# First q, k and cache fetches of each attention stage on ScalarE's queue, and the work pool below the k and q pools

## The chip, the cores and the metric

The kernel runs on one core of a Trainium2 chip. The time is device microseconds of one launch. Five engines work side by side, each in its own order: TensorE (PE, matmuls), VectorE (DVE), ScalarE (ACT), GpSimd (POOL) and SyncE (SP, which only issues transfers). Transfers between HBM and SBUF are issued here by SP and, for a few outputs, by ACT.

## What the kernel must compute

One inference step of a two layer encoder for 2048 frames of a new stream and 64 frames of a running one, whose 256 past frames of keys and values come from a cache. Each layer is x + W_out(silu(gate) * mixer(RMSNorm(x))), with one input projection to q, k, v and gate. There are 4 heads of width 256, and the model is 1024 wide. Layer 0 mixes by differential attention, layer 1 by stick-breaking attention:

```python
# layer 0, per head: two softmax maps of 128 wide queries and keys
p = softmax(where(visible, q @ k * 128**-0.5, NEG_INF))   # two maps m
w = p[:, :, 0] - lam * p[:, :, 1]
o = w @ v
# layer 1
z = q @ k * 256**-0.5
a = where(earlier, exp(z + rev_cumsum(log_sigmoid(-z))), 0)
o = a @ v
```

New k and v rows are outputs too, and a final RMSNorm follows layer 1.

## The kernel before

All data lie transposed, features on the partitions. Float32 operands are split into a high and a low part (`split`, L47: ACT writes `hi`, at L49; DVE or POOL subtracts, at L50), and a product is three matmuls (`mm3`, L54 to L56). Each layer has three stages, one after the other:

- **p_phase** projects q, k, gate and v per head. The last projection of a layer is v of head 3: 17 blocks of 24 matmuls. Per block ACT evacuates the PSUM tile to a work tile `o1` or `o2` (L240), issues the store `out_v` on its own queue (L241) and makes the high part of the split tile `s` (L49); POOL makes the low part (L50); SP stores it to `vS` in HBM (L190). The split tiles have two buffers, `o1` and `o2` two each.
- **a_phase** runs over groups of four blocks of 128 queries (and, per head, first the 64 sample rows). `load` fetches q and k of a group (tiles `q`, `k`) from HBM, `values` fetches v, `past` the cache. In layer 0 the scores `s` go from PSUM to SBUF on DVE (L404, which also writes the small tile `st`), the exponentials run on ACT (L412), and the combined row is transposed on PE (`tp`, L468), split into `wh` and `wl` and multiplied with v (`o`). In layer 1 ACT evacuates the scores (tile `z`, L438). PSUM holds three score tiles. `mixed` (and in layer 0 `finish`, L525 to L538) normalises and gates a finished group in the tiles `sq`, `rm`, `rs` and `ot`, and SP stores `ot` to `oT` in HBM (L538, L544).
- **o_phase** reads `oT` back in chunks `oraw` of 128 features (three buffers, L709), splits each into `oh` and `ol` and multiplies with the output weights `wh`, `wl` (split from `wraw`, L697) into `ps`. It starts with the 512 frames of the attention's first two groups of frames; the frames of the last group come later. The second block of frames uses the other pair of `oh`, `ol`.

The program is written with tile pools: a pool takes a stretch of SBUF when it is opened, pools are stacked in the order in which they are opened, and a stage's pools lie over those of the stage before. A tile that lies over an older one waits until all readers and writers of the old one are done, transfers included. The instructions of each engine are put in order before the run, by a planner inside the framework that simulates the queues; so a change in one wait can move instructions elsewhere. SP and ACT share eight completion counters in turn: a new transfer waits until the transfer eight issues earlier has landed.

In the kernel before, all q, k, v and cache fetches are issued on SP (L336, L350, L372). The pools of the attention stage lie in the order v, weights `wh`/`wl`, gate, k, q, rows, and the work pool with `st`, `osc`, `sq`, `rm`, `rs`, `ot` last. The tile of the first k lies there over a work tile `o1` of the projection. The output stage of layer 0 opens a pad of 36 KB per partition first (L672).

Of the kernel before, what the change touches and what calls it, by code (L numbers as in the profile page):

```python
# [42 lines left out]
def pool(tc, name, bufs=1, **kw):  # L43
    return tc.tile_pool(name=name, bufs=bufs, reuse_waits="tile", **kw)


def split(nc, hi, lo, x, lo_eng):  # L47

    nc.scalar.activation(hi, x, AF.Copy)  # L49
    lo_eng.tensor_tensor(lo, x, hi.bitcast(F32), ALU.subtract)  # L50
# [263 lines left out]
def a_phase(tc, k, layer):  # L314
    nc = tc.nc
    ck, cv = k.ckT[layer], k.cv[layer]
    with ExitStack() as es:
        vp = es.enter_context(pool(tc, f"av{layer}", 4))
        wtp = es.enter_context(pool(tc, f"awt{layer}", 3))
        gp = es.enter_context(pool(tc, f"ag{layer}"))  # L320
        kp = es.enter_context(pool(tc, f"ak{layer}", 4))
        qp = es.enter_context(pool(tc, f"aq{layer}", 2))
        rbp = es.enter_context(pool(tc, f"arb{layer}", 2))
        rap = es.enter_context(pool(tc, f"ara{layer}", 8))
        wk = es.enter_context(pool(tc, f"aw{layer}", 1))
        psp = es.enter_context(pool(tc, f"aps{layer}", 2, space=PSUM))
        osc = None
        if layer == 0:
# [7 lines left out]
        def past(src, hi, lo):  # L336

            raw = qp.tile([P, 2, PAST], F32, tag="raw", name="raw", bufs=2)
            nc.sync.dma_start(out=raw, in_=src)
            split(nc, hi, lo, raw, nc.gpsimd)  # L340

        def rows(ap, h, c0, c1):
# [2 lines left out]
        def head_rows(ap, h, c0, c1):  # L345
            return ap[h * HW:(h + 1) * HW, :, c0:c1].rearrange("(m p) s t -> p s m t", p=P)

        def fetch(dst, src):
            for s in range(2):
                nc.sync.dma_start(out=dst[:, s], in_=src[:, s])  # L350

        def load_q(h, t0, n):
            t, hl = pair(qp, f"q{n}", [2, n], 2 if n == 512 else 1)
            fetch(t.bitcast(F32), head_rows(k.qS[layer], h, t0, t0 + n))
            return hl

        def load_k(h, g):
            t, hl = pair(kp, "k", [2, 512])
            if g is None:
                past(rows(ck, h, 0, PAST), t[:, 0, :, :PAST], t[:, 1, :, :PAST])  # L360
                fetch(t[:, :, :, PAST:PAST + NS].bitcast(F32), head_rows(k.kS[layer], h, SEQ, T))
            else:
                fetch(t.bitcast(F32), head_rows(k.kS[layer], h, g * 512, g * 512 + 512))
            return hl

        def load_v(h, g):
            hs = slice(h * HW, (h + 1) * HW)
            t, hl = pair(vp, "v", [4, HW])
            vs = k.vS[layer]
            if g is None:  # L370
                past(cv[:, hs].rearrange("(b p) e -> p b e", p=P), t[:, 0, :2], t[:, 1, :2])
                nc.sync.dma_start(out=t[:NS, :, 2].bitcast(F32), in_=vs[SEQ:T, :, hs])  # L372
            else:
                fetch(t.bitcast(F32), vs[g * 512:g * 512 + 512, :, hs].rearrange("(b p) s e -> p s b e", p=P))
            return hl
# [176 lines left out]
        def sums():  # L552
            return wk.tile([P, 4], F32, tag="s15", name="s15", bufs=4) if layer == 0 else None

        def load(i):
            if i < len(groups) and i not in loaded:
                h, g = groups[i]
                qt = load_q(h, SEQ, NS) if g is None else load_q(h, g * 512, 512)
                loaded[i] = (qt, load_k(h, g))
# [5 lines left out]
        def group(h, rows, s15, nq, kbs, wq, t0):  # L565
            u = K()
            u.last = (h, t0) == (H - 1, 3 * 512)
            u.h, u.rows, u.s15, u.nq, u.kbs, u.wq, u.t0, u.wts = h, rows, s15, nq, kbs, wq, t0, {}
            return u

        def all_units():
            for i, (h, g) in enumerate(groups):
                load(i)
                load(i + 1)
                qt, kt = loaded[i]
                if g is None:
                    row = rap.tile([P, 320], F32, tag="rs", name="rowS", bufs=1)
                    s15 = sums()
                    m, r = unit(row, 0, NS, qt, [(kt, PAST + NS, PAST + NS)], None if layer == 0 else k.smask, s15)
                    yield m, r, group(h, [row], s15, NS, [(i, 0, P, 0), (i, 1, P, 0), (i, 2, NS, 0)], NS, SEQ)  # L580
                    continue
                base = i - g
                full = [(loaded[base + c][1], 512, 512) for c in range(g)]
                per = {0: 4, 1: 2}.get(g, 1)
                wid = {0: 512, 1: 1024, 2: 2048, 3: 2048}[g]
                u_rows, s15 = [], sums()
                kbs = [(base + c, b, P, 0) for c in range(g) for b in range(4)]
                kbs += [(i, b, P, b) for b in range(4)]
                for j in range(4):
                    if j % per == 0:  # L590
                        slot = rap.tile([P, 2048], F32, tag="ra", name="rowA")
                    row = slot[:, (j % per) * wid:(j % per) * wid + wid]
                    u_rows.append(row)
                    m, r = unit(row, j, P, qt, full + [(kt, (j + 1) * P, max(256, (j + 1) * P))], k.mask[layer], s15)
                    yield m, r, group(h, u_rows, s15, P, kbs, 512, g * 512) if j == 3 else None

        def s_stream():

            prev, note = iter(()), None
            for m, r, nt in all_units():  # L600
                live = [m, prev]
                cost = [0.0, 0.0]
                while any(x is not None for x in live):
                    n = min((x for x in range(2) if live[x] is not None), key=lambda x: cost[x])
                    try:
                        c = next(live[n])
                        cost[n] += c
                        yield c
                    except StopIteration:
                        live[n] = None  # L610
                if note:
                    ready.append(note)
                prev, note = r, nt
            yield from prev
            ready.append(note)
# [134 lines left out]
def trunk(ctx: ExitStack, tc, xT, wqkg, wv, wo, small, ckT, cv, rope, masks, idn,  # L750
# [52 lines left out]
    with pool(tc, "rs0", side="right") as rp:  # L803
        p_phase(tc, k, 0, xT, rstd_tiles(rp))
    a_phase(tc, k, 0)
    with pool(tc, "rs1", side="right") as rp:
        rs = rstd_tiles(rp)
        k.acc = rp.tile([P, TT[0][1]], F32, name="acc")
        o_phase(tc, k, 0, xT, rs)
        p_phase(tc, k, 1, k.y1T, rs)  # L810
    a_phase(tc, k, 1)
    o_phase(tc, k, 1, k.y1T, None)

# [73 lines left out]
```

## Time and profile before

| | before |
|---|---|
| three runs | 2995.58, 3002.43, 3003.42 us |
| median | 3002.43 us |
| profiled execution | 3003.18 us, of which the span from the first to the last instruction is 3001.4 us |
| PE busy | 2888.2 us (96%) |
| DVE, ACT, POOL busy | 1683.0 us (56%), 1246.1 us (42%), 873.7 us (29%) |
| mean granted TensorE clock | 0.98 of full speed |

The stages follow one another: projection of layer 0 to 779 us, its attention to 1343 us, output and projection of layer 1 to 2285 us, its attention to 2801 us, and the output stage to the end. In the table "busy" is the time in which an engine executes; waiting is not in it. PE is the engine to watch: what it does not do at full clock is lost.

### The profile page before, as it was taken

How to read it: one execution, taken by the hardware profiler on the slowest of the kernel's cores; microseconds unless marked ns; L12 is line 12 of the kernel's file. 1: busy time of each engine (PE TensorE's matmuls, PEld its weight loads, DVE VectorE, ACT ScalarE, POOL GpSimd, SP SyncE). 2: the span in 40 equal slices, each digit the busy share in tenths (PEclk: the TensorE clock that was granted, in tenths of full speed). 3: DMA queues.
4: the chain of work that ended last, by engine and by line, in shares of the span. 5: the costliest groups of instructions: out<-in, count | busy, mean ns of one | idle time of the engine just before them, and what ended most of it. 6: DMA issues, size and time to landing. Idle time of an engine off the chain costs nothing.

```text
span 3001.4 us, 44967 instructions
## 1 busy us (share of the span) xinstructions
PE 2888.2 (96%) x16424; PEld 2514.3 (84%) x16424; DVE 1683.0 (56%) x2968; ACT 1246.1 (42%) x2499; POOL 873.7 (29%) x949
## 2 busy tenths in 40 slices
PE   8999999999799999989999999999997999999998
PEld 7888998989677777767899888989897778888788
DVE  8754625346288877764355225033252978878454
ACT  5312222212366665654243122222113877777433
POOL 4533333333133444444004223223221000001221
PEclk9999999999899999999999999999998999999999
DMA  5476456354715443326354443443427344433442
GB/s 166 152 197 184 141 160 184 130 155 121 245 60 180 137 133 116 114 93 227 115 161 132 150 142 109 135 143 121 138 91 255 118 150 137 133 128 131 134 150 96
DMA packets 345950, 432.20 MB, mean 144 GB/s; under 512 B 48768, under 2 KB 232320, under 8 KB 345728
## 3 DMA queue, kind: packets, MB, share of 16 engines
q1 hardware_dynamic: 325936, 411.47, 42.8%
q10 hardware_dynamic: 19792, 17.85, 1.8%
q8 instruction: 129, 2.11, 0.3%
q14 instruction: 93, 0.76, 0.1%
HBM read 236.73 MB, written 192.48 MB: 143 GB/s over the span
## 4 chain that ended last, share of the span: by engine, by line
PE 53%; DVE 12%; ACT 5%; DMA 3%; issue 3%; SPq 1%; POOL 1%; DVEq 0%; ACTq 0%; POOLq 0%
PE pj L55 8%; PE pj L54 8%; PE pj L56 8%; DVE rowA L452 4%; PE ps L55 3%; PE ps L56 3%; PE ps L54 3%; PE o L54 3%; PE o L56 3%; PE o L55 3%; PE tp L468 2%; PE s L54 2%; DVE rowA L449 2%; PE s L56 2%; PE s L55 2%
## 5 line engine op out<-in xcount | busy, mean ns | idle before, releaser
L54 PE MATMUL pj<-hl,whi 128*128 128x512 f32 (+2 forms) x1920 | 679.6, 354 | 2.2 <-ACT whi L49 1.9
L55 PE MATMUL pj<-hh,wlo 128*128 128x512 f32 (+2 forms) x1920 | 677.5, 353 | 0.1
L56 PE MATMUL pj<-hh,whi 128*128 128x512 f32 (+2 forms) x1920 | 677.0, 353 | 0.0
L49 ACT ACTIVATE s<-o 128x256 fp32r<-128x256 f32 (+2 forms) x424 | 164.6, 402 | 638.5 <-DVE o L226 196.6
L54 PEld LDWEIGHTS pj<-hl,whi 128*128 128x128 f32 x1920 | 363.2, 189 | 48.0 <-ACT whi L49 2.1
L55 PEld LDWEIGHTS pj<-hh,wlo 128*128 128x128 f32 x1920 | 363.2, 189 | 45.8 <-issue 0.7
L56 PEld LDWEIGHTS pj<-hh,whi 128*128 128x128 f32 x1920 | 363.0, 189 | 45.0
L50 POOL TENSOR_TENSOR s<-o,s 128x256 fp32r<-128x256 f32 (+2 forms) x280 | 202.3, 730 | 555.2 <-ACT s L49 530.2
L54 PE MATMUL pj<-wlo,hh 128*128 128x256 f32 (+1 forms) x1088 | 309.2, 286 | 14.5 <-ACT hh L144 7.6
L54 PE MATMUL s<-k,q 128*128 128x512 f32 (+3 forms) x656 | 270.9, 413 | 48.4 <-DMA k<-kS 33.7
L55 PE MATMUL pj<-whi,hl 128*128 128x256 f32 (+1 forms) x1088 | 310.4, 286 | 1.6 <-DVE hl L145 1.6
L56 PE MATMUL pj<-whi,hh 128*128 128x256 f32 (+1 forms) x1088 | 309.9, 285 | 0.0
L54 PE MATMUL o<-wl,v 128*128 128x512 f32 (+4 forms) x688 | 269.4, 392 | 11.5 <-DVE wl L50 8.2
L56 PE MATMUL o<-wh,v 128*128 128x512 f32 (+4 forms) x688 | 250.2, 364 | 0.0
L55 PE MATMUL o<-wh,v 128*128 128x512 f32 (+4 forms) x688 | 249.2, 362 | 0.0
L56 PE MATMUL s<-k,q 128*128 128x512 f32 (+3 forms) x656 | 245.6, 374 | 0.0
L55 PE MATMUL s<-k,q 128*128 128x512 f32 (+3 forms) x656 | 245.3, 374 | 0.0
L50 DVE TENSOR_TENSOR wl<-tp,wh 128x512 fp32r<-128x512 f32 (+5 forms) x344 | 195.2, 576 | 83.8 <-ACT wh L49 83.1
L54 PE MATMUL ps<-ol,wh 128*128 128x512 f32 (+2 forms) x640 | 227.7, 356 | 3.9 <-ACT wh L49 3.9
L55 PE MATMUL ps<-oh,wl 128*128 128x512 f32 (+2 forms) x640 | 229.9, 359 | 1.5 <-DVE wl L50 1.1
L56 PE MATMUL ps<-oh,wh 128*128 128x512 f32 (+2 forms) x640 | 227.5, 355 | 0.0
L226 DVE SCALAR_TENSOR_TENSOR o<-pj,rs 128x512 f32<-128x512 f32 (+2 forms) x80 | 47.8, 597 | 320.1 <-PE pj L56 319.9
(164 smaller groups left out, 5664.2 us busy)
## 6 DMA issues: line engine op xcount, KB each, us to landing
vS<-s SPq DMA_DIRECT2D x128, 256.0 KB, 2.5
q<-qS SPq DMA_DIRECT2D x64, 512.0 KB, 5.0
v<-vS SPq DMA_DIRECT2D x64, 512.0 KB, 5.1
k<-kS SPq DMA_DIRECT2D x64, 512.0 KB, 8.1
wraw<-in_wqkg SPq DMA_DIRECT2D x96, 256.0 KB, 3.5
out_v<-o ACTq DMA_DIRECT2D x128, 128.0 KB, 1.9
qS<-s SPq DMA_DIRECT2D x128, 128.0 KB, 2.4
kS<-s SPq DMA_DIRECT2D x128, 128.0 KB, 2.4
```

What stands on the lines that cost most here:

```text
L49: nc.scalar.activation(hi, x, AF.Copy)
L50: lo_eng.tensor_tensor(lo, x, hi.bitcast(F32), ALU.subtract)
L54: nc.tensor.matmul(ps, lh, rl, start=start, stop=False, skip_group_check=True)
L55: nc.tensor.matmul(ps, ll, rh, start=False, stop=False, skip_group_check=True)
L56: nc.tensor.matmul(ps, lh, rh, start=False, stop=stop, skip_group_check=True)
L226: nc.vector.scalar_tensor_tensor(o, ps, -0.5 / 16 if qk == 0 else -0.5, rbc[ti], ALU.mult, ALU.mult)
L449: nc.vector.scalar_tensor_tensor(rr, zz, 0.0, rr, ALU.min, ALU.subtract)
L452: nc.vector.tensor_tensor_scan(rv, z[:nq, c1:c0:-1], rv, r[:nq, c1:c1 + 1] if done else 0.0, ALU.add, ALU.subtract)
L468: nc.tensor.transpose(tp[:kn, j * P:j * P + u.nq], u.rows[j][:u.nq, i * P:i * P + kn], k.idn[:u.nq, :u.nq])
```

## The change

Two edits in `a_phase`. The fetches go through a variable `queue[0]`, which is ACT's queue while `load(0)` and `load(1)` run and SP's afterwards; these two calls now come ahead of the loop. They cover the sample rows' q, the first group's q, both k tiles and the cache's k of head 0: nine transfers per layer. v, the cache's v and all later groups stay on SP. And the work pool is opened before the k and q pools.

```diff
         gp = es.enter_context(pool(tc, f"ag{layer}"))
+        wk = es.enter_context(pool(tc, f"aw{layer}", 1))
         kp = es.enter_context(pool(tc, f"ak{layer}", 4))
         qp = es.enter_context(pool(tc, f"aq{layer}", 2))
         rbp = es.enter_context(pool(tc, f"arb{layer}", 2))
         rap = es.enter_context(pool(tc, f"ara{layer}", 8))
-        wk = es.enter_context(pool(tc, f"aw{layer}", 1))
...
             raw = qp.tile([P, 2, PAST], F32, tag="raw", name="raw", bufs=2)
-            nc.sync.dma_start(out=raw, in_=src)
+            queue[0].dma_start(out=raw, in_=src)
...
+        queue = [nc.scalar]
+
         def fetch(dst, src):
             for s in range(2):
-                nc.sync.dma_start(out=dst[:, s], in_=src[:, s])
+                queue[0].dma_start(out=dst[:, s], in_=src[:, s])
...
         def all_units():
+            load(0)
+            load(1)
+            queue[0] = nc.sync
             for i, (h, g) in enumerate(groups):
                 load(i)
                 load(i + 1)
```

What this does to the order of instructions is seen at three places. The first is the queue of SP at the end of layer 1's projection. `vS` is the store of a split v block (s_21876 is the last of them), `v` a value tile, `k` a key tile, `ckT` and `cv` the cache. Before:

```order
L190 DMA vS_71<-s_21812 256x1x256
L190 DMA vS_71<-s_21844 256x1x256
L372 DMA v<-vS_71 64x2x256
L350 DMA v<-vS_71 128x4x256 x4
L190 DMA vS_71<-s_21876 256x1x256
L499 DMA g<-gT_73 128x2x64
L350 DMA v<-vS_71 128x4x256 x2
L339 DMA raw<-in_ckT 128x2x256
L350 DMA k<-kS_68 128x2x64 x2
L350 DMA k<-kS_68 128x2x512 x6
```

Now, on ACT's queue (o_21713 and o_21745 are the twelfth and thirteenth of the 17 blocks):

```order
L339 DMA raw<-in_ckT 128x2x256
L352 DMA q_21927<-qS_66 128x2x512
L240 ACTIVATE o_21713<-pj,rc_13445 128x256
L352 DMA q_21927<-qS_66 128x2x512
L241 DMA out_v<-o_21713 128x256
L49 ACTIVATE s_21716<-o_21713 128x256
L240 ACTIVATE o_21745<-pj,rc_13445 128x256
L49 ACTIVATE k<-raw 128x2x256
L352 DMA k<-kS_68 128x2x512
L241 DMA out_v<-o_21745 128x256
L49 ACTIVATE s_21748<-o_21745 128x256
L352 DMA k<-kS_68 128x2x512
```

The first q, k and cache tiles are issued between the blocks of v, some blocks before the projection ends, where they stood behind the last v store and the v loads. The same holds in layer 0.

The second place is SP's queue at the end of layer 0's projection, where s_7517 and s_7581 are the third from last and the last split block. Before:

```order
L190 DMA vS_70<-s_7485 256x1x256
L190 DMA vS_70<-s_7517 256x1x256
L190 DMA vS_70<-s_7549 256x1x256
L372 DMA v<-vS_70 64x2x256
L350 DMA v<-vS_70 128x4x256 x4
L190 DMA vS_70<-s_7581 256x1x256
```

And now:

```order
L374 DMA v<-vS_70 64x2x256
L352 DMA v<-vS_70 128x4x256 x3
L352 DMA k<-kS_67 128x2x512
L190 DMA vS_70<-s_7485 256x1x256
L352 DMA k<-kS_67 128x2x512
L352 DMA v<-vS_70 128x4x256 x3
L352 DMA q_8210<-qS_65 128x2x64
L190 DMA vS_70<-s_7517 256x1x256
L352 DMA q_8210<-qS_65 128x2x64
L339 DMA raw<-in_cv 128x2x256
L190 DMA vS_70<-s_7549 256x1x256
L190 DMA vS_70<-s_7581 256x1x256
```

The last four v stores moved behind k and v loads of the attention. The work pool of layer 0 lies now over a work tile `o1` of the projection: DVE's first score copy (which writes `st`) and ACT's `osc` wait for the store of s_7517 to land, for the split of s_7581 on POOL that follows it, and for the last `out_v` stores.

The third place is ACT's queue at the end of layer 0's attention, with what each row waits for in brackets (DMAHW a transfer's completion counter). `oh` is the high part of the output stage's first block of frames, `wh` with a number a weight of the output stage, `whi` a weight of the next projection, `wh` from `tp` a transposed row block, and the `ot` row belongs to the group before the last. Before:

```order
L506 ACTIVATE ot<-o,osc 128x512
L49 ACTIVATE oh<-oraw 128x512 [waits DMAHW1_49,DMAHW0_49]
L49 ACTIVATE oh<-oraw 128x512 [waits DMAHW2_49]
L49 ACTIVATE oh<-oraw 128x512 [waits DMAHW3_49]
L49 ACTIVATE wh<-tp 128x512 [waits PE_49] x2
L49 ACTIVATE wh<-tp 128x512 [waits PE_49,Activation_49,Pool_49]
L49 ACTIVATE oh<-oraw 128x512 [waits DMAHW6_49]
```

And now:

```order
L49 ACTIVATE wh_13610<-wraw 128x512 [waits DMAHW6_49]
L49 ACTIVATE whi<-wraw 128x512 [waits DMAHW7_49]
L49 ACTIVATE oh<-oraw 128x512 [waits DMAHW0_49,Pool_49]
L49 ACTIVATE oh<-oraw 128x512 x2
L49 ACTIVATE wh_13652<-wraw 128x512 [waits DMAHW4_49]
L49 ACTIVATE wh_13652<-wraw 128x512 [waits DMAHW6_49]
L49 ACTIVATE oh<-oraw 128x512 [waits DMAHW7_49]
```

The eight `oh` stood inside the attention's tail, before the transposed row blocks of the last group. They are now behind all of it, and behind the last group's `finish` (whose rows on ACT end ten rows above the first one shown), since their tile lies over `ot`: the first waits (DMAHW0, Pool) for the store of the last group's `ot` to land. PE's first matmul of the output stage waits for the `ol` made from it. In layer 1 `oh` overlaps `ot` by 1 KB per partition and waits for the last group's store in the same way. Of the eight `oraw` chunks three are fetched ahead of that wait (there are three buffers), the other five after it. In both layers the weights of the output stage's first columns are now split ahead of `oh`.

## Rows read from the trace of the kernel before

**Rows 1.** PE timeline, first scores (start, duration, instruction, [idle before, releaser])

```profile
795.68 0.50 PE L54 MATMUL s<-k,q 128*64 128x320 f32 x1 [16.59 <-DMA k<-kS]
...
2300.33 0.50 PE L54 MATMUL s<-k,q 128*64 128x320 f32 x1 [15.77 <-DMA k<-kS]
```

**Rows 2.** Windows, layer 1's start (busy us by engine, clock, DMA share, GB/s)

```profile
2272.00:2282.00 10.00, 10.00 (x85) 10.00 (x84) 0.00 (x0) 3.25 (x8) 3.23 (x5) 1.00 0.53 184
2290.00:2300.00 10.00, 0.00 (x0) 0.00 (x0) 0.00 (x0) 0.00 (x0) 0.69 (x1) 0.50 1.06 345
2300.00:2305.00 5.00, 4.09 (x16) 3.30 (x17) 1.01 (x3) 1.62 (x4) 0.00 (x0) 0.50 1.05 387
```

**Rows 3.** Timeline of SP's queue at both starts

```profile
789.14 6.28 SPq L350 DMA_DIRECT2D k<-kS  x8
...
2293.76 6.27 SPq L350 DMA_DIRECT2D k<-kS  x8
```

**Rows 4.** Transfers of the page (KB each, us to landing)

```profile
vS<-s SPq DMA_DIRECT2D x128, 256.0 KB, 2.5
...
k<-kS SPq DMA_DIRECT2D x64, 512.0 KB, 8.1
```

**Rows 5.** Windows, layer 0's start

```profile
755.00:765.00 10.00, 10.00 (x85) 10.00 (x85) 0.00 (x0) 1.92 (x5) 1.48 (x2) 1.00 1.02 342
785.00:795.00 10.00, 0.00 (x0) 0.00 (x0) 0.00 (x0) 0.00 (x0) 0.00 (x0) 0.50 1.07 346
795.00:805.00 10.00, 8.52 (x34) 6.61 (x34) 6.15 (x39) 4.51 (x19) 0.29 (x1) 0.50 1.05 384
```

**Rows 6.** Timeline of POOL and DVE, last v split, first score copy

```profile
781.42 0.72 POOL L50 TENSOR_TENSOR s<-o,s 128x256 fp32r<-128x256 f32 x1
...
796.75 0.48 DVE L404 TENSOR_SCALAR_CACHE_REDUCE rowS<-s 64x320 f32<-64x320 f32 x1 [55.74 <-PE s L56]
```

**Rows 7.** Timeline, end of layer 0's attention, five engines

```profile
1345.60 1.10 PE L521 MATMUL ss<-sq,ones 128*128 128x512 f32 x2 [2.27 <-DVE sq L513]
1346.13 0.82 PE L54 MATMUL ps<-ol,wh 128*128 128x512 f32 x1
...
1358.54 1.73 POOL L50 TENSOR_TENSOR wlo<-wraw,whi 128x512 fp32r<-128x512 f32 x1
...
1363.79 1.73 POOL L537 TENSOR_TENSOR ot<-ot,g 128x512 f32<-128x512 f32 x1
...
1365.55 0.38 SPq L538 DMA_DIRECT2D oT<-ot  x1
...
1368.89 1.66 ACT L49 ACTIVATE oh<-oraw 128x512 fp32r<-128x512 f32 x3
...
1370.42 0.69 DVE L50 TENSOR_TENSOR ol<-oraw,oh 128x512 fp32r<-128x512 f32 x1 [6.05 <-DMA oT<-ot]
```

**Rows 8.** Transfers issued in 1364 to 1372 and 2798 to 2804

```profile
oT<-ot SPq DMA_DIRECT2D x1, 512.0 KB, 4.8
...
oT<-ot SPq DMA_DIRECT2D x1, 512.0 KB, 4.5
```

**Rows 9.** Timeline of DVE and PE, tail of layer 0's attention

```profile
1310.29 3.43 DVE L50 TENSOR_TENSOR ol<-oraw,oh 128x512 fp32r<-128x512 f32 x2
...
1314.38 0.80 PE L54 MATMUL o<-wl,v 128*128 128x512 f32 x1 [3.04 <-DVE wl L50]
```

**Rows 10.** Waits of PE, 1340 to 1400 (us in total, times, longest)

```profile
PE ps L54 <- ACT wh L49: 2.1, 2, 1.8
```

**Rows 11.** Window in the output stage of layer 0

```profile
1390.00:1395.00 5.00, 4.64 (x12) 3.48 (x13) 2.79 (x5) 1.86 (x4) 1.28 (x1) 0.66 0.64 224
```

**Rows 12.** Timeline of PE and DVE, end of layer 1's attention

```profile
2801.48 0.40 PE L54 MATMUL ps<-ol,wh 128*128 128x512 f32 x1
...
2801.32 1.29 DVE L543 TENSOR_TENSOR ot<-o,g 128x512 f32<-128x512 f32 x2 [0.49 <-PE o L56]
2802.52 0.68 DVE L50 TENSOR_TENSOR ol<-oraw,oh 128x512 fp32r<-128x512 f32 x1
```

## The prediction

> **What bounds the kernel now.** PE is busy 96% of the span, so a change gains or loses what it takes off PE's idle time and off its clock. I read PE's waits first: the two longest are the first score matmuls of the two attentions, each waiting for the first k, 16.59 us in layer 0 and 15.77 us in layer 1 [rows 1]. Then SP's queue: those k loads are issued at 789 and 2294 us, ten microseconds after the projection ends [rows 3], behind the last v store and the v loads. Then the windows: in layer 1 the transfers took 53% of the DMA engines at 184 GB/s before the end of the projection, and all of them at 345 GB/s in the gap; the clock granted in the gap and until 2305 is 0.50, the lower of the two levels [rows 2]. In layer 0 the transfers were at 342 to 384 GB/s, 102 to 107% share, already from 755 to 765 and again from 785 to 805 [rows 5]. Last I read the other end of each attention, since the moved work pool changes what the output stage lies over: there PE goes on without a break, at 1346.13 and 2801.48 [rows 7, 12], and this is what I think the change breaks.
>
> The profiled execution takes 3003.18 us for a span of 3001.4, and is 0.75 us above the median; the sum is made on it and then lowered by 0.75. A difference of 0.3%, 9 us, is about what a measurement of this kernel can tell from no change.
>
> **Start of layer 1: 13 us gained (6 to 17).** PE's last projection matmul is done at 2284.56 (2300.33 less 15.77). Now k of the sample rows and q stand between v blocks on ACT's queue, and the first k of group 0 after block 13, about four blocks before the end; they are there, or nearly, when PE comes free. What is late next is the first evacuation `z`: ACT issues the last `out_v` before it, and that waits for the counter of the v store of block 13, which stands on SP behind k loads of the next group. Nine early transfers on ACT and five on SP, mostly of 512 KB [rows 4], move into the 17 us before the end. At 345 GB/s instead of 184 [rows 2] 17 us have room for 2.7 MB more; about 4.5 MB want in, so the rest, 1.8 MB or 5 us, hangs over the end. PE has three score tiles to fill meanwhile. I take 3.5 us idle of the 15.8, a gain of 12.3, and of the 2.0 us that 4.09 us of work at half clock cost [rows 2] about 1. Low end: the store lands after a k load's 8.1 us [rows 4] and the clock falls as before, 15.8 - 8.1 - 1.5 = 6. High end: no gap and no lost clock, 15.8 + 2.0 = 17 after a small start.
>
> The Trainium skill has a rule against this gain (DMA: Bandwidth & Descriptors, section Issuing engines are not separate DMA queues): transfers issued by different engines run on the same 16 DMA engines, and a second issuer saves only issue time. By it alone the gain would be the issue of eight k loads, 6.3 us [rows 3]. I go by the rows in layer 1, where engines stood half free and the gain comes from an earlier place in the order; in layer 0 the rows agree with the rule.
>
> **Start of layer 0: nothing (5 lost to 8 gained).** The same fetches go out earlier, but the score copy on DVE now waits for the last v split, since `st` lies over `o1`. That split waits for the store of s_7517, and this stands on SP behind the fourth k tile and three v tiles; behind the copy on DVE stand all later score copies, and PE stops after three score tiles. From about 763 on (some six blocks of 24 matmuls, 2.8 us each by the 85 in 10 us of [rows 2], before the projection's end at 795.68 less 16.59), 18 transfers of 512 KB (two q, four k, three v pairs) and some 3.2 MB of smaller ones must move before that store lands: 12.6 MB at 342 to 384 GB/s [rows 5] are 33 to 37 us, so it lands at 796 to 800. The split adds POOL's 0.72 us [rows 6] and ACT's part, taken as long. The first copy thus starts at 797 to 801, against 796.75 now [rows 6]: 0 to 4 us later, but with more of k and v loaded. I take 0. ACT's early issues also wait on counters, while the projection runs; a block takes 2.8 us, and the stage's eight PSUM tiles cover some 20 us, so I cost this at nothing; it becomes the third rival if that cover is gone.
>
> **End of layer 0's attention: 20 us lost (12 to 28).** Now `oh` lies over `ot`. Before, `oh` and `ol` were split inside the attention's tail and PE began `ps` at 1346.13, right behind `ss` [rows 7]; the `finish` of the last group went on beside it until POOL's last product at 1363.79 and the store at 1365.55. The trace of before has the same wait already, for the second block of frames: its `ol` sat 6.05 us until the store landed, and ran at 1370.42 [rows 7]. With the landing of 4.8 us [rows 8] the store is there at 1370.3; then `oh` 0.55 (1.66 for three) and `ol` 0.69 [rows 7], and PE starts at 1371.6: 25.5 us of nothing, since PE's queue holds nothing else. The order of `finish` and of the weight splits between its steps on POOL and ACT is the same as before, so I take this length. A fixed landing cost plus size, as the Trainium skill has it (DMA: Bandwidth & Descriptors, section Anatomy of one DMA: about 2.0 us + bytes / 436 GB/s, measured for another issue path), would be 3.2 us instead of the trace's 4.8, an estimate that takes 1.6 us off; the trace's row stands.
>
> After such a gap the clock is at half for about 4 us of work, as in [rows 2]: +2. Against that: without the `ol` of 3.43 us on DVE the wait of 3.04 us in the tail [rows 9] shrinks, -2.5; and the weights of the first columns are split during the gap, so the 2.1 us wait for them [rows 10] and the half-clock window behind it, 0.34 x 4.64 = 1.6 [rows 11], go, with 1 us of small waits: -4.7. Sum 25.5 + 2 - 2.5 - 4.7 = 20. Low end: two or three weight splits like the 1.73 us one on POOL [rows 7] no longer in the way and a landing of 2.5 us as for `vS` [rows 4], 8 us less. High end: nothing is given back, and the five `oraw` chunks fetched late cost some waits, 28.
>
> **End of layer 1's attention: 9 us lost (5 to 14).** PE started `ps` at 2801.48 without waiting; the two `ot` products end at 2802.6 [rows 12]; a landing of 4.5 us [rows 8] is 2807.1, `oh` 0.55 and `ol` 0.68 more: 2808.4, 7 us idle. +2 for the clock. The late five chunks each take a landing behind the y loads; PE has three to four weight columns to work on, so I add nothing, and 5 us at the high end.
>
> **Sum.** -13 + 0 + 20 + 9 = +16: 3003.2 + 16 - 0.75 = 3018 us.
>
> **Rivals.** (1) Not slower: the v stores in layer 0 drain as early as now, because SP isn't held by the counters; the last split was on POOL at 781.42 [rows 6]. If the store of s_7517 lands by 784, the copy starts at about 785: 12 us gained and 4.3 us of half clock [rows 5], together 16, and the sum is 0: 3002. The point is whether that store lands before 788; against it speak the full transfers from 785 to 805 [rows 5]. (2) The chain behind `finish` is quick, since PE's idling leaves DVE, ACT and POOL to it: the low ends of both boundaries, 12 and 5, give +4: 3006. For it: POOL's part is long only by splits put in between. Against: the order of these is unchanged. With the high gain in layer 1 it would reach 3002; both (1) and (2) together, 2990. (3) ACT blocks on its early transfers: a k load takes 8.1 us to land [rows 4], and the next issue on the same counter holds all v evacuations behind it; the projection ends some 5 us later in each layer. Sum +26: 3028. For it: ACT's queue now waits for k and q to land between blocks. Against: the PSUM tiles. The skill's rule, with only 6.3 us won in layer 1, ends at 3025 and counts here.
>
> **Chances and range.** Forecast 0.52, (1) 0.14, (2) 0.14, both together 0.06, (3) with the rule 0.14. Of the forecast and (3) 0.03 falls below 3011.4, of (2) 0.01 above it. Slower by over 0.3%: 0.64. Faster by over 0.3%, below 2993.4: both together and a little of (1), 0.08. Within: 0.28. The range from 2998 to 3033 leaves out the faster cases and the high ends of all terms at once. The likeliest case alone spans 3008 to 3030.
>
> **What would show it.** Right: PE's gap at 2285 is 2 to 6 us and its clock stays at 1.00 for most of it; the first score copy in layer 0 is near 797 with PE stopped after three score tiles; a gap of 18 to 26 us between the last `ss` of layer 0 and `ps`, released by `ol`, and one of 5 to 9 us in layer 1. Wrong: a first copy before 790, or a boundary in layer 0 of under 12 us; or projection blocks on which PE waits for a PSUM tile.

## The result and the profile after

The changed kernel is slower: 3026.44 us (median of four runs, 3024.30 to 3028.07) against 3000.36 us (median of four, 2995.58 to 3003.42) beside it, a ratio of 1.0088 with a 95% interval of 1.0070 to 1.0105. The profiled execution takes 3026.12 us for a span of 3024.0 us, 22.6 us more than before. The forecast, slower and 3018 us, has the right side, and the time is inside the range (2998 to 3033).

PE's waits in the whole trace (instruction, what it waited for, us in total, times, longest us):

```profile
PE ps L54 <- DVE ol L50: 29.9, 2, 23.7
PE s L54 <- DVE rowS L406: 20.9, 1, 20.9
PE s L54 <- ACT z L440: 11.8, 6, 4.0
```

The waits of the first scores for k [rows 1] are gone, and each has a successor: `rowS` in layer 0, `z` in layer 1. The first row is new and is the two ends of the attentions.

Where the span went, in us (projection 0, attention 0 with its start, the gap behind it, output 0 with projection 1, attention 1 with its start, the gap behind it, output 1). The marks between them are the starts of matmuls: the last of a projection, the last `o` of an attention, the first `ps` of an output stage. So the gap of layer 0 also holds the two `ss`:

| | proj. 0 | att. 0 | gap | out. 0, proj. 1 | att. 1 | gap | out. 1 | span |
|---|---|---|---|---|---|---|---|---|
| before | 778.8 | 564.2 | 3.1 | 938.2 | 517.1 | 0.1 | 199.9 | 3001.4 |
| after | 779.4 | 563.7 | 28.0 | 932.7 | 514.7 | 6.5 | 199.0 | 3024.0 |
| difference | +0.6 | -0.6 | +24.9 | -5.4 | -2.4 | +6.4 | -0.9 | +22.6 |

**End of layer 0's attention**, against [rows 7]: timeline of PE, POOL, SP, ACT and DVE (start us, busy us, engine, line, instruction, in brackets the idle time before it and its releaser).

```profile
1343.03 0.28 PE L56 MATMUL o<-wh,v 128*128 128x256 f32 x1
1345.58 1.75 PE L523 MATMUL ss<-sq,ones 128*128 128x512 f32 x2 [2.27 <-DVE sq L515]
1371.02 0.79 PE L54 MATMUL ps<-ol,wh 128*128 128x512 f32 x1 [23.68 <-DVE ol L50]
...
1362.12 1.26 POOL L539 TENSOR_TENSOR ot<-ot,g 128x512 f32<-128x512 f32 x1
...
1364.81 0.42 SPq L540 DMA_DIRECT2D oT<-ot  x1
...
1369.56 1.67 ACT L49 ACTIVATE oh<-oraw 128x512 fp32r<-128x512 f32 x3 [0.72 <-DMA oT<-ot]
...
1370.23 0.74 DVE L50 TENSOR_TENSOR ol<-oraw,oh 128x512 fp32r<-128x512 f32 x1 [6.30 <-ACT oh L49]
```

Read upwards, this is the chain forecast: `ps` waits for `ol`, `ol` for `oh`, `oh` for the store of `ot` to land, and that store for POOL's last product, which starts 17 us behind `ss`. The transfers issued around it give the landing (KB, us):

```profile
oT<-ot SPq DMA_DIRECT2D x1, 512.0 KB, 4.7
```

What comes back is in the output stage, against [rows 11]. The first 5 us behind the gap run at half clock; after that PE has no wait, and its windows are full, at full clock:

```profile
1371.00:1376.00 5.00, 4.98 (x12) 3.92 (x13) 2.07 (x2) 2.12 (x4) 2.77 (x3) 0.50 0.94 335
1391.00:1411.00 20.00, 20.00 (x90) 16.57 (x89) 8.71 (x12) 5.84 (x10) 2.58 (x2) 1.00 0.70 225
```

The kernel before also lost some clock there, behind the wait for `ss`:

```profile
1346.00:1351.00 5.00, 5.00 (x15) 3.71 (x14) 2.13 (x3) 3.48 (x7) 1.28 (x1) 0.66 0.62 202
```

**End of layer 1's attention**, against [rows 12]: SP, DVE and PE, and a window behind the gap.

```profile
2819.69 0.38 SPq L546 DMA_DIRECT2D oT<-ot  x1
...
2824.21 0.69 DVE L50 TENSOR_TENSOR ol<-oraw,oh 128x512 fp32r<-128x512 f32 x1 [2.44 <-ACT oh L49]
...
2824.96 0.80 PE L54 MATMUL ps<-ol,wh 128*128 128x512 f32 x1 [6.26 <-DVE ol L50]
...
2825.00:2831.00 6.00, 6.00 (x15) 4.70 (x16) 1.95 (x2) 2.00 (x4) 2.34 (x2) 0.53 0.92 281
```

**Start of layer 0's attention**, against [rows 1, 5, 6]: timeline of PE, POOL and DVE, then two windows (busy us of PE, PEld, DVE, ACT, POOL, with the number of instructions in brackets, granted clock, DMA share, GB/s).

```profile
779.48 0.30 PE L54 MATMUL s<-k,q 128*64 128x320 f32 x1
...
782.06 0.23 PE L385 MATMUL s<-mb,idb 128*128 128x128 bf16 x1
803.23 0.58 PE L54 MATMUL s<-k,q 128*128 128x256 f32 x1 [20.93 <-DVE rowS L406]
...
801.92 0.72 POOL L50 TENSOR_TENSOR s<-o,s 128x256 fp32r<-128x256 f32 x1 [5.99 <-ACT s L49]
...
802.68 0.48 DVE L406 TENSOR_SCALAR_CACHE_REDUCE rowS<-s 64x320 f32<-64x320 f32 x1 [64.87 <-POOL s L50]
...
785.00:795.00 10.00, 0.00 (x0) 0.00 (x0) 0.00 (x0) 0.55 (x2) 0.72 (x1) 0.56 1.08 362
795.00:805.00 10.00, 1.77 (x8) 1.59 (x9) 1.80 (x16) 1.86 (x7) 1.44 (x2) 0.50 0.79 250
```

PE starts 0.1 us after the projection, fills three PSUM tiles by 782 and stands until 803. The first copy is at 802.68, right behind the last v split on POOL; before it was at 796.75 [rows 6]. The half clock, though, ends sooner than before. The kernel before and the changed one, from 795 and from 803 on:

```profile
795.00:811.00 16.00, 14.52 (x54) 11.33 (x54) 8.87 (x51) 5.96 (x23) 0.29 (x1) 0.50 0.82 293
...
803.00:811.00 8.00, 7.78 (x41) 6.26 (x41) 7.08 (x48) 5.39 (x23) 0.28 (x1) 0.78 0.40 111
```

PE's work at half clock in the first 100 us of the stage cost 7.2 us before and 1.7 now (half of PE's busy time in the stretches granted 0.50), while its idle time rose from 18.4 to 23.1 us.

**Start of layer 1's attention**, against [rows 1, 2]: PE and ACT, then the attention in three windows.

```profile
2303.88 0.30 PE L54 MATMUL s<-k,q 128*64 128x320 f32 x1
2308.17 0.39 PE L54 MATMUL s<-k,q 128*128 128x256 f32 x1 [3.12 <-ACT o L240]
...
2309.64 0.43 ACT L440 ACTIVATE z<-s 64x320 f32<-64x320 f32 x1 [1.22 <-DMA vS<-s]
...
2303.80:2353.80 50.00, 35.95 (x175) 28.79 (x173) 30.61 (x42) 34.87 (x69) 6.21 (x15) 0.90 0.66 221
2353.80:2403.80 50.00, 49.95 (x273) 41.93 (x272) 45.78 (x54) 41.66 (x69) 4.01 (x10) 1.00 0.34 110
sum 514.60, PE 490.46 PEld 408.61 DVE 401.55 ACT 367.79 POOL 34.86; mean PE 163.49 PEld 136.20 DVE 133.85 ACT 122.60 POOL 11.62
```

The same windows of the kernel before, counted from its last projection matmul:

```profile
2284.30:2334.30 50.00, 33.38 (x189) 27.87 (x188) 22.69 (x40) 25.76 (x55) 5.41 (x13) 0.83 0.82 271
2334.30:2384.30 50.00, 46.96 (x244) 38.44 (x243) 45.85 (x52) 42.52 (x70) 1.98 (x8) 1.00 0.15 49
sum 517.10, PE 485.81 PEld 405.15 DVE 401.92 ACT 370.06 POOL 39.36; mean PE 161.94 PEld 135.05 DVE 133.97 ACT 123.35 POOL 13.12
```

PE starts scores 16 us sooner, yet in the first 50 us it is busy only 2.6 us more (and gets through 175 matmuls instead of 189). What it waits for in these 50 us is room for the next scores in PSUM, which ACT has to clear by evacuating scores (`z`) and the projection's last v blocks (`o` of L240):

```profile
PE s L54 <- ACT z L440: 10.9, 5, 4.0
PE s L54 <- ACT o L240: 3.1, 1, 3.1
```

Idle time and work at half clock together cost 19.1 us of the first 50 in both kernels: 16.6 and 2.5 before, 14.1 and 5.0 now. Over the whole attention PE idles 24.1 instead of 31.3 us, but is busy 490.5 instead of 485.8: of 7.1 us less idling, 4.7 go into longer busy time, 4.0 of them into half clock (11.6 against 7.6 us).

### The profile page after: what moved, and what is told of

Same layout as the page of the kernel before. It is cut to its first block, busy times and chain, and to the rows that moved or that the text cites. A ratio compares the mean times of both kernels' runs of the same rounds, so it can differ in the third digit from the quotient of the medians.

```text
span 3024.0 us, 44956 instructions
## 1 busy us (share of the span) xinstructions
PE 2892.1 (96%) x16424; PEld 2516.2 (83%) x16424; DVE 1682.2 (56%) x2968; ACT 1247.6 (41%) x2499; POOL 874.4 (29%) x949
## 4 chain that ended last, share of the span: by engine, by line
PE 42%; DVE 7%; ACT 3%; DMA 1%; issue 1%; POOL 0%; DVEq 0%; SPq 0%; ACTq 0%; POOLq 0%
PE pj L56 8%; PE pj L55 8%; PE pj L54 8%; PE ps L54 4%; PE ps L56 4%; PE ps L55 4%; DVE rowA L454 3%; DVE rowA L451 2%; PE o L54 1%; PE o L56 1%; PE o L55 1%; ACT rowA L448 1%; DVE wl L50 1%; ACT rowA L450 1%; PE tp L470 1%
## 5 line engine op out<-in xcount | busy, mean ns | idle before, releaser
L54 PE MATMUL s<-k,q 128*128 128x512 f32 (+3 forms) x656 | 270.0, 412 | 48.4 <-DVE rowS L406 20.9
L54 PE MATMUL o<-wl,v 128*128 128x512 f32 (+4 forms) x688 | 269.3, 391 | 10.9 <-DVE wl L50 7.0
L49 ACT ACTIVATE wh<-tp 128x512 fp32r<-128x512 f32 (+5 forms) x344 | 170.1, 507 | 138.2 <-PE tp L470 124.2
```

Of the source, the lines that this page charges most:

```text
L54: nc.tensor.matmul(ps, lh, rl, start=start, stop=False, skip_group_check=True)
```

## Experiments

Every kernel was timed beside the kernel before, and its ratio is to that one. That kernel's own times spread from 2986 to 3005 us in 19 executions, so differences of a few us between medians of different versions are read with their intervals, and a stage's length comes from one trace. The stages of all of them, in us:

| | proj. 0 | att. 0 | gap | out. 0, proj. 1 | att. 1 | gap | out. 1 | time | ratio (95%) |
|---|---|---|---|---|---|---|---|---|---|
| e1 pools alone | 778.9 | 556.1 | 28.5 | 931.5 | 512.6 | 6.6 | 197.7 | 3013.22 | 1.0042 (1.0027 to 1.0057) |
| e2 queue alone | 779.7 | 567.1 | 3.1 | 935.8 | 519.7 | 0.1 | 201.2 | 3007.33 | 1.0026 (1.0017 to 1.0036) |
| e3 `oh` moved | 778.4 | 565.5 | 5.3 | 934.2 | 511.1 | 0.1 | 199.5 | 2996.32 | 0.9993 (0.9980 to 1.0006) |
| e4 and `st` moved | 777.9 | 553.1 | 5.4 | 933.8 | 512.7 | 0.1 | 200.1 | 2984.42 | 0.9945 (0.9930 to 0.9960) |
| e5 e4, all on SP | 779.2 | 548.9 | 5.3 | 934.0 | 511.4 | 0.1 | 199.7 | 2981.04 | 0.9935 (0.9919 to 0.9951) |
| e6 and `wl` moved | 779.0 | 552.8 | 5.4 | 932.9 | 513.4 | 0.1 | 199.6 | 2984.78 | 0.9946 (0.9928 to 0.9964) |
| e7 e6, all on SP | 776.7 | 549.3 | 5.3 | 932.8 | 509.5 | 0.1 | 199.3 | 2976.63 | 0.9923 (0.9903 to 0.9942) |
| e8 e7, three `z` | 777.9 | 549.1 | 5.3 | 932.8 | 505.6 | 0.1 | 199.7 | 2972.73 | 0.9909 (0.9894 to 0.9923) |
| e9 e6, ScalarE in layer 1 only | 778.5 | 549.3 | 5.4 | 932.9 | 513.4 | 0.1 | 199.4 | 2980.66 | 0.9936 (0.9919 to 0.9953) |

**e1 and e2: each half of the change by itself.** e1 moves the work pool and leaves all fetches on SP; e2 puts the first fetches on ScalarE's queue and leaves the pools.

```diff
 # e1
         gp = es.enter_context(pool(tc, f"ag{layer}"))
+        wk = es.enter_context(pool(tc, f"aw{layer}", 1))
         kp = es.enter_context(pool(tc, f"ak{layer}", 4))
...
-        wk = es.enter_context(pool(tc, f"aw{layer}", 1))
 # e2
...
-                nc.sync.dma_start(out=dst[:, s], in_=src[:, s])
+                queue[0].dma_start(out=dst[:, s], in_=src[:, s])
...
+            load(0)
+            load(1)
+            queue[0] = nc.sync
```

Expected of e1: 

> Only the second edit: the work pool lies below k and q, all fetches stay on SP's queue. Theory (the loss at the ends of the attentions comes from the work pool's place): the gap before the first output matmul is 22 to 26 us in layer 0 and 5 to 8 us in layer 1 as with both edits, the loss there some 25 us net, and with the starts of the attentions changed by -5 to +5 us the time is 3020 to 3031 us. Rival (the loss comes from the queue, through the planner's other order): no such gaps, 2995 to 3005 us.

Expected of e2: 

> Only the first edit: nine fetches per layer on ScalarE's queue, pools as before. Theory: no gaps at the ends of the attentions; the first k still lies over o1, so it is fetched after the last v split, but no longer behind the v loads; each of the two waits for k falls from 16 us to 8 to 12 us: 2985 to 2998 us. Rival (ScalarE's queue order is what loses): gaps of over 5 us at an attention's end or PE waiting for PSUM tiles in the projection, 3010 us or more.

PE's waits of e1:

```profile
PE ps L54 <- DVE ol L50: 31.1, 2, 24.8
PE s L54 <- DVE rowS L404: 21.2, 1, 21.2
```

And PE's first scores in layer 1 of e1, with a row of SP's queue before the end of layer 0's projection:

```profile
2295.05 0.28 PE L56 MATMUL pj<-whi,hh 128*128 128x256 f32 x1
2295.17 0.30 PE L54 MATMUL s<-k,q 128*64 128x320 f32 x1
...
752.57 1.10 SPq L350 DMA_DIRECT2D k<-kS  x2
```

SP's queue in the kernel before, at the same place:

```profile
752.13 1.31 SPq L350 DMA_DIRECT2D q<-qS  x2
753.49 0.46 SPq L339 DMA_DIRECT2D raw<-in_ckT  x1
```

PE's waits of e2, and ACT's queue there:

```profile
PE s L54 <- DMA k<-kS: 32.1, 2, 16.2
...
789.25 5.97 ACTq L352 DMA_DIRECT2D k<-kS  x4
```

At both starts, the pools did what I had put down to the queue. With the first k no longer over `o1`, SP itself fetches it from 752.57 on, 26 us before the projection ends, and the first scores follow the projection by 0.12 us in both layers. The description of the change was wrong on one point: the first q and cache tile did not stand behind the v loads in the kernel before; SP fetched them from 752 on in layer 0 and from 2256 on in layer 1, and only k was late.

With the queue edit alone k still comes late: PE waits 16.18 and 15.88 us, as before [rows 1], and the time of 3007 us missed the expected 2985 to 2998. My 8 to 12 us took it that k would be rid of the v loads on ACT's queue, and it isn't. ACT issues the first k of layer 0 at 789.25, as late as SP did [rows 3], 0.02 us after the landing of a v load that SP had issued at 781.84; the trace has it waiting for that load's completion counter, and SP and ACT share these counters. The first k of layer 1 waits for a v load in the same way, at 2295.01.

Both ends, 28.5 and 6.6 us, belong to the pools, as forecast; e2 has none. e1 as a whole came out under its expected 3020 to 3031 us, since its attentions are 8.1 and 4.5 us shorter than before, where I had allowed 5 us for both.

**e3: `oh` off the work pool.** The change with both edits, but with three weights of layer 0's output stage in a pool of their own below, and small pads, so that the first `oh` no longer lies over `ot`.

```diff
+            wlp = es.enter_context(pool(tc, f"olw{layer}"))
+            es.enter_context(pool(tc, f"opad2{layer}")).tile([P, 808], F32, name="pad2")
             yp = wk = es.enter_context(pool(tc, f"ok{layer}", 3))
+        if last:
+            es.enter_context(pool(tc, "opad1")).tile([P, 256], F32, name="pad1")
...
-            hi = wp.tile([P, NC, P], F32R, name=f"wh{s}")
-            lo = wp.tile([P, NC, P], F32R, name=f"wl{s}")
+            hi = (wp if last or s < 7 else wlp).tile([P, NC, P], F32R, name=f"wh{s}")
+            lo = (wp if last or s < 6 else wlp).tile([P, NC, P], F32R, name=f"wl{s}")
```

Expected: 

> Both edits, and the output stage's oh moved off the attention's work pool (layer 0: three weight tiles of 12 KB and a pad of 3.2 KB below it; layer 1: a pad of 1 KB). Theory: both gaps at the ends go; with the 24.9 - 5.4 us and 6.5 - 0.9 us that they cost net, 3026 falls to 2999 to 3003 us, no better than before, since the starts of the attentions gave only 2 to 3 us. Rival (the gap is the finish chain itself, which the next waits would show anyway): over 3012 us.

Timeline of PE at the end of layer 0's attention in e3:

```profile
1348.19 2.05 PE L523 MATMUL ss<-sq,ones 128*128 128x512 f32 x2 [4.02 <-DVE sq L515]
1349.25 1.42 PE L54 MATMUL ps<-ol,wh 128*128 128x512 f32 x1
```

Both gaps are gone and the median is 30 us lower than with the change, level with before and 3 us under the expected range. The wait for `rowS` stays, at 22.2 us. So the loss of the change hangs on where `oh` lies.

**e4 and e5: `st` off the work pool.** e4 is e3 with the small tiles `st`, `osc` and `s15` in a pool above the row tiles, so that the first score copy waits for nothing of the projection; e5 is e4 with all fetches on SP.

```diff
+        stp = es.enter_context(pool(tc, f"ast{layer}", 1))
...
-            osc = wk.tile([P, 2], F32, name="osc")
+            osc = stp.tile([P, 2], F32, name="osc")
...
-            st = wk.tile([P, 16], F32, tag="st", name="st", bufs=16)[:nq]
+            st = stp.tile([P, 16], F32, tag="st", name="st", bufs=16)[:nq]
...
 # e5
-        queue = [nc.scalar]
+        queue = [nc.sync]
```

Expected of e4: 

> As e3, and st, osc and s15 in a small pool of their own above the row tiles, so that the first score copy of layer 0 waits for no v split. Theory (the place of st over o1 is what keeps layer 0 from gaining): PE's wait of 20.9 us behind rowS falls below 8 us, 2984 to 2992 us. Rival (the DMA engines are full there, so that the next wait is for k or v): the wait moves to another row and the time stays within 4 us of e3.

Expected of e5: 

> As e4 (oh off the work pool, st in a pool of its own), but all fetches on SP: what ScalarE's queue is worth once the work pool's costs are out of the way. Theory (the free place of the first k tile makes the early fetch, not the queue): layer 0's start stays without a long wait, and the time is within 8 us of e4's 2984. Rival (the early fetch needs ScalarE's queue): a wait of over 10 us for k in layer 0 or 1, 2995 us or more.

Windows of e4 at the start of layer 0's attention:

```profile
775.00:785.00 10.00, 7.21 (x55) 6.42 (x55) 2.95 (x23) 4.50 (x17) 1.97 (x2) 1.00 1.07 378
785.00:795.00 10.00, 8.90 (x41) 6.19 (x40) 8.37 (x51) 6.11 (x20) 0.72 (x1) 0.83 1.08 371
```

From 785 to 795, where PE did nothing in the kernel before nor in the changed one, it is busy 8.90 us at a clock of 0.83, and the attention is 12.4 us shorter than in e3: the wait through the small tiles in the work pool was what ate the gain of the early k, and the time is as expected. The transfers run at 371 GB/s with a share of 1.08 while PE works, so PE was not waiting for them to clear. e5, whose median is 3.4 us lower, within the noise of the two, shows that early places on SP's queue serve as well.

**e6, e7 and e9: `wl` off the projection's tiles, and the queue again.** In layer 1 of the changed kernel the first transposed block's `wl` came 40 us after the first scores; it lay over `o2`. e6 is e4 with the gate and work pools moved down and `wh`, `wl` up behind a pad (the pads of the output stages are set to match); e7 is e6 with all on SP; e9 has ScalarE's queue in layer 1 only.

```diff
+        es.enter_context(pool(tc, f"apad{layer}")).tile([P, 2816 if layer else 512], F32, name="apad")
+        wtp = es.enter_context(pool(tc, f"awt{layer}", 3))
...
 # e7                               # e9: queue = [nc.scalar if layer else nc.sync]
-        queue = [nc.scalar]
+        queue = [nc.sync]
...
```

Expected of e6: 

> As e4, and the tiles wh and wl of the attention moved off the projection's work tiles o2, o1 and s2 (the gate and work pools lie there instead, used later). Theory (in layer 1 the first o matmuls come 57 us after the projection's end, against 39 before, because wl lies over o2 and waits for the last v splits, behind loads on SP): the first 30 o matmuls of layer 1 are done by 40 us, and its attention, 512.7 us from the last projection matmul to the last attention matmul, falls by 5 to 12 us: 2972 to 2980 us. Rival (the attention is bound by its row work on DVE and ACT, whatever PE starts with): the o matmuls come earlier but the attention keeps its length within 3 us, 2981 to 2988 us.

Expected of e7: 

> As e6 with all fetches on SP. Theory: within 8 us of e6, so that the queue is worth no more than the other order of the rest costs or gives. Rival: ScalarE's queue is worth the issue of its nine fetches twice, 10 us or more in its favour.

Expected of e9: 

> The version with the free weight tiles, with the first fetches on ScalarE's queue in layer 1 only; layer 0 fetches on SP. With the queue edit in both layers it took 2984.8 us, in neither 2976.6; of the 8.1 us the traces put 5.7 into layer 0 (2.2 before its projection ends, 3.5 in its attention) and 4.0 into layer 1's attention, with 1.6 given back between. Theory (each layer pays for its own early fetches, by the order that the planner then gives the rest of that attention): layer 0 as with SP (attention 549 to 550 us), layer 1's attention 512 to 514 us, the kernel 2979 to 2982 us. Rival (the difference is in layer 0, and layer 1 only follows): 2975 to 2978 us with a layer 1 attention of 509 to 510 us.

e6 took the wait away and gained nothing, as its rival has it. The first `o` of layer 1 comes 13 us after the projection instead of 45 in e4, though the 30th at 50 us, not by the 40 expected, and in the first 50 us PE's waits for `z` (9.8 us in e4) are gone. In their place it waits for finished rows:

```profile
PE tp L472 <- ACT rowA L462: 5.7, 3, 3.7
PE s L54 <- ACT o L240: 2.8, 1, 2.8
PE o L54 <- DVE ot L547: 2.1, 1, 2.1
```

Attention 1 did not get shorter (513.4 against 512.7 us), so the place of `wl` was not what set its length.

In no pair does the queue gain. By the medians it costs 13.2 us (e1 to the change), about 8 (before to e2, by its ratio of 1.0026), 3.4 (e5 to e4) and 8.1 (e7 to e6, a little over the 8 expected). The first two are clear of the noise; the intervals of the last two pairs overlap. e9 came out as its theory has it: with ScalarE's queue in layer 1 alone, attention 0 is that of e7 (549.3 us) and attention 1 that of e6 (513.4 us). By these traces each layer pays for its own early fetches, some 4 us (4.2 and 1.3 in the pair of e4 and e5), and not at the start, where the first scores follow the projection by 0.1 us either way.

**e8: a third `z`.** e7 with three buffers for `z` in layer 1; the sample's row goes below the gate pool and the pad is that much shorter.

```diff
+        rsp = es.enter_context(pool(tc, f"ars{layer}"))
...
-        rbp = es.enter_context(pool(tc, f"arb{layer}", 2))
+        rbp = es.enter_context(pool(tc, f"arb{layer}", 3 if layer else 2))
```

Expected: 

> The version with the free weight tiles and everything on SP (2977 us), with three instead of two buffers for the z tile of layer 1 (the row of the sample block goes to the lower pad, which is made that much shorter, so that the other tiles keep their places apart from the row buffers). Question: why layer 1's attention takes 509.5 us although its scores no longer wait at the start. Theory (the scores run into the two z buffers: TensorE idles some 9 us in the first 50 us because the next z waits for a row to finish): with a third buffer TensorE is busy over 44 of the first 50 us instead of 41, and the attention shortens by more than 5 us, to 504 or less; the kernel to about 2971 us. Rival (the rows themselves come at the pace of the exchange between ScalarE and VectorE, whatever the number of z buffers): the attention stays within 3 us of 509.5 us and the kernel within 2974 to 2980 us.

Windows of layer 1's attention in e7 (first 50 us, and from 100 us to the end):

```profile
2264.10:2314.10 50.00, 41.16 (x210) 33.52 (x208) 34.53 (x47) 36.37 (x74) 6.36 (x17) 0.90 0.73 245
...
2364.10:2773.60 409.50, 398.02 (x2174) 332.23 (x2173) 325.03 (x418) 293.04 (x521) 30.09 (x88) 0.99 0.40 133
```

The same in e8:

```profile
2265.20:2315.20 50.00, 42.06 (x209) 34.13 (x208) 33.94 (x49) 37.00 (x76) 6.96 (x15) 0.90 0.74 249
...
2365.20:2770.80 405.60, 397.78 (x2173) 332.98 (x2174) 320.32 (x417) 291.69 (x520) 26.95 (x87) 0.99 0.39 131
```

Neither theory holds as stated. The attention shortens by 3.8 us, between the two, and not where I looked: the first 50 us hold 42.06 instead of 41.16 us of PE and no more matmuls, while the idle time after the first 100 us falls from 11.5 to 7.8 us. The premise was wrong: in e7 PE waits only 0.8 us for `z` in the first 50 us, and 5.9 for the rows of its transposes. Nor are the 3.8 us shown to be waits for `z`: after the first 100 us these take 0.8 us in e7, and most of what goes is waits for `wl` (5.6 to 2.8 us), in an order that the planner made anew. e8 has the lowest median, 0.9% under the kernel before, though its interval overlaps that of e7.

## Why the prediction was right, and which step failed

| term | forecast | measured | from |
|---|---|---|---|
| start of layer 1 | -13 | -2.4 | attention 1 |
| start of layer 0 | 0 | +2.0 | projection 0 +0.6, attention 0 -0.6, without the 2.0 us of its tail |
| end of layer 0 | +20 | +17.5 | gap +24.9, output and projection -5.4, tail -2.0 (PE's wait for `wl` of 3.04 us [rows 9] is 1.0 us) |
| end of layer 1 | +9 | +5.5 | gap +6.4, output -0.9 |
| sum | +16 | +22.6 | |

**Ends of the attentions: right.** The mechanism is the one forecast, link by link, and the gap of 24.9 us is the 25.5 us that [rows 7, 8] gave. e3 shows it: with `oh` elsewhere both gaps go. The sums came out 2.5 and 3.5 us lower. The half clock behind each gap is there (0.50 and 0.53 in the windows above, 2.8 and 2.9 us of PE's time in the two output stages), but more comes back than I had counted: in the output stage of layer 0 the kernel before lost 3.0 us idle and 3.4 us to half clock, of which my sum had no term for the 1.7 us behind `ss` (0.66 from 1346 to 1351); in that of layer 1 PE idles 10.4 instead of 12.9 us. The rest, under 2 us in each stage, I can't place.

**Start of layer 0: the wait right, the size in part luck.** The copy waited for the last v split, PE stopped after three tiles, and the copy came at 802.68, 1.7 us behind the forecast 797 to 801: the store of s_7517 landed at 801.35, where I had 796 to 800. e4 shows the cause. But PE went on 7.5 us later than before (803.23 against 795.68), and the stage lost only 2 because PE's work at half clock cost 1.7 us instead of 7.2. My term had no clock in it.

**Start of layer 1: the step that failed** is "I take 3.5 us idle of the 15.8, a gain of 12.3, and of the 2.0 us that 4.09 us of work at half clock cost about 1". The gain is 2.4 us, below even the low end of 6. Its first half happened: k was there, PE started at once, and the first `z` was held by the store of a v block, 5.8 us after the first score. But the step has PE go on at the pace of before once `z` runs, and it does not: it idles 14.1 us of the first 50 instead of 3.5, 10.9 of them for the next `z` and 3.1 for the evacuation of the projection's last blocks, and half clock takes 5.0 us instead of 2.5 where I had 1 us coming back. So the first 50 us gain nothing.

Its `s` matmuls run far ahead, the first 60 within 16 us of the projection's end instead of 31, but the first 30 of `o` stand at 57 us instead of 39: scores ahead do not help while `o` has to wait, for a free `wl` here, and for finished rows where `wl` is free (e6). More room for scores does not help, either: in e8 PE's waits for `z` are down to 0.6 us (2.0 in e7, 11.8 in the changed kernel), and it is busy 42 us of the first 50.

The whole still came inside the range because the range is wide and the misses partly cancel: 10.6 us too much gain here and 2.0 at layer 0's start, against 6.0 us too much loss at the ends.

**The cause of the gain, too, was wrongly placed:** I gave it to the queue, and e1 and e2 show that it is the pools. This did not change the side of the sum, since both edits were made together, but "an earlier place in the order" comes from the address that is free, not from ScalarE. The Trainium skill's rule against the queue (DMA: Bandwidth & Descriptors, section Issuing engines are not separate DMA queues: all issuers share the same 16 engines, so a second one saves only issue time) was the better guide: in no pair here does the second issuer gain, and by the medians it costs 3 to 13 us. That cost is more than the rule says.

**Rivals.** (1) is out: the copy was 18 us later than the 785 it needs. (2) is out: the chain behind `finish` is as long as forecast. (3) is nearest in time, with 3028 us, but not by its mechanism: ACT does wait for q and k in the projection (9.7 us at the end of layer 1's), yet projection 0 ends only 0.6 us later. The 12 us between the spans of e1 and the change lie mostly in the attentions (7.5 and 2.0 us), not in the projections.

**Still open.** Why ScalarE's queue lengthens the rest of the attention: with the queue the planner's order of all later instructions changes as well, and no run held that order fixed. The loss has no one form: of the 7.5 us in attention 0 between e1 and the change, 4.4 are work at half clock and 2.1 idle time, while of the 3.9 us in attention 1 between e7 and e6 idle time makes more than all (4.5). And why the rows of layer 1 take as long from a start with k at hand: neither the free `wl` (e6) nor a third `z` (e8) freed them.

## What to carry to other kernels

Before moving a pool, list for every tile at a stage's start and end which older tile lies under it and which store must land before that one is free; here, by address alone, an operand of the output stage (`oh`) cost PE 25 us of waiting, the small tile of a score copy 12 us, and the first k a wait of 16 us in each layer, of which the stages kept only a part. When a gap at a stage's start goes, ask what the engine that waited will do after its first few instructions, and when the inputs of that work can be there: here PE ran ahead with scores and then waited nearly as long for ACT and DVE.

## What the runs showed of the hardware

A stuttering PE loses twice, by idling and by working at the lower clock. In layer 1's first 50 us it worked in pieces, and the granted clock was 0.90 on average (0.86 from 2329 to 2354), a mix of the two levels, and 5.0 us went to the lower one; 175 matmuls took 35.95 us there, and the next 273, without pauses, 49.95 us at 1.00. In layer 0, where PE stood for 20.9 us, the clock was 0.50 from 795 to 805, though the scores came back at 803. The transfers at layer 0's start ran at 362 to 378 GB/s, with a share above 1, with PE idle (the changed kernel, 785 to 795) as with PE busy (e4, 775 to 795). A transfer issued on ACT can wait for one issued on SP: in the version with the queue edit alone, ACT issued the first k of each layer only when a v load of SP's had landed, 7.3 to 7.4 us after its issue, since the two queues of this program share their completion counters.
